# Odd layer of a hybrid trunk: the recurrences of two heads run together, 8 chunks per product stage

## The chip, the cores and the metric

The kernel runs on one core of a Trainium2 chip. The core's engines work from instruction queues of their own, each in its own order: TensorE (PE; its weight loads are shown as PEld), VectorE (DVE), ScalarE (ACT), GpSimd (POOL) and SyncE (SP), which here issues the DMA transfers. Engines wait for one another through semaphores. The metric is the device time of one launch in microseconds, lower is better.

## The reference, cut to what matters

Two layers on 512 tokens of width 1024, batch 1. The even layer (a short convolution beside a gated DeltaNet) and what follows each layer (output projection, LayerNorm, a gated embedding) stay as they are. The odd layer is an HGRN2 recurrence with 16 heads of width 128:

```python
q_raw, f_raw, i_in, z = jnp.split(x @ w_in, 4, axis=-1)
f = lower_bound + (1.0 - lower_bound) * jax.nn.sigmoid(f_raw)
q = jax.nn.silu(q_raw)
k = 1.0 - f
# per head: S_t = diag(f_t) S_{t-1} + k_t v_t^T,  o_t = S_t^T q_t,  with v = i_in
o = hgrn2_recurrence(q, k, i_in, log f)
o = rms_norm(o, hgrn_norm_g) * jax.nn.silu(z)
return o.reshape(bsz, s, 2048) @ w_out
```

## The kernel before

Everything is held feature-major: features on the 128 partitions, the 512 tokens (`S`) on the free axis. A weight chunk of 128 x 1024 (512 KB) is loaded by SP, then split into a high part (`whi`, ScalarE, L96) and a low part (`wlo`, VectorE, L97); three buffers of each (`chunk`). A dense product runs in three passes, hi*hi, hi*lo, lo*hi (`mm3`, L104 to L106). `proj` makes one 128 x 512 output of 8 such triples.

**The odd layer** goes head by head (`odd_layer`). `hgrn_front` projects f (`pf`) and q (`pq`), for every second head the values of two heads (`pi`, two chunks, token-major, 256 columns per product), and the output gate z (`pz`). `hgrn_core` then makes the attention inside each chunk of 128 tokens (`C`; four chunks, `NCH`) by doubling blocks, and the recurrence over chunks. Its TensorE work per head:

- `products` (L736), called three times (once on `q`, for B = 2 and 8 on `X`): inside each block of 32 tokens, keys times 48 columns, 16 products of 128 rows on 32 columns, at four column tiles in turn. The results `pw` are picked into `AD` by VectorE (L740).
- `pl` (L798), B = 32 and 64: four products per left block of each pair of blocks, on 32 or 64 columns; for B = 32 there are two left blocks (columns 0 and 64), each followed by a copy into `AT` (L799). A product of plain float32 shows as two instructions in the trace.
- three transposes `pkt` (L806), then per chunk the outputs `o` (L813, L814) and the state's increment `dS` (L817), all 128 wide.
- `head_norm`: squares, a normalisation, four transposes `pot` (L540), the gate, and the split into `yh` and `yl`.

Between them VectorE multiplies Q and k by the decays of ever larger blocks (`merge`, `total`, L719).

**Order.** The core is a generator. `start` queues it, and each triple of dense products calls `pump`, which emits the next stage once the number of triples that the stage yielded (`HG`; `HN` for the normalisation) has gone by. `drain` emits all that is left up to a head. So recurrence stages of one head are emitted between the dense triples of the next head's front. The framework's planner then sets each engine's final order, by what it takes to be ready first among emitted work, so a stage can end up later than emitted. On the chip each engine runs its queue in that order.

Of the kernel before, what the change touches and what calls it, by code (L numbers as in the profile page):

```python
"""Two-layer hybrid trunk (gated short convolution || gated DeltaNet, then HGRN2) on one core.

Everything is kept feature-major ([feature on partitions, token on the free axis]).  The large
products run as three float32r passes over exact hi/lo splits of both operands.
"""
# [17 lines left out]
P = 128  # L23
D = 1024
KD = D // P          # 8 feature tiles of the residual stream
S = 512
C = 128              # recurrence chunk
NCH = S // C
H = 8                # DeltaNet heads
HH = 16              # HGRN heads  # L30
# [7 lines left out]
HG = 5, 5, 2, 3, 2  # L38
# [5 lines left out]
# columns of the packed small parameters  # L44
# [3 lines left out]
class K:  # L48
    def __init__(self, tc, ctx, a):
# [4 lines left out]
        # work emitted between the steps of the dense products: [steps to wait, pieces]  # L54
# [21 lines left out]
    def po(self, name="po"):  # L76
        return self.ps.tile([P, 512], F32, tag="po", name=name, bufs=1)

    def chunk(self, src):
        """One weight chunk [128, 8, 128]: load, then split it exactly into hi + lo."""  # L80
        ch = self.chunk_tiles()
        self.chunk_part(ch, src, slice(0, 1024))
        return ch[1:]
# [15 lines left out]
    def mm3(self, ps, terms, first=True, last=True):  # L99
        """ps = sum over terms of (wh + wl)^T (xh + xl), without the lo*lo product."""  # L100
# [13 lines left out]
    def pump(self, units=1):  # L114
        """Emit what is due of the waiting work behind `units` more steps of dense products."""
# [15 lines left out]
    def drain(self, h=99, lanes=3):  # L131
        """Emit the waiting work of the heads up to h."""
# [6 lines left out]
    def rsqrt(self, pool, v, shape, tag):  # L139
        """1/sqrt(v) for v > 0: exponent-halving seed and three Newton steps."""  # L140
# [15 lines left out]
    def constants(self):  # L156
# [18 lines left out]
        # sums from the middle of the chunk, and from its start: [j, (2, i)]  # L175
        self.UCT = cp.tile([P, 2, P], F32, name="UCT")
        UC, UT = self.UCT[:, 0], self.UCT[:, 1]
        # [j, i] = 1 where j <= i
        sel(UT, self.ones, [[1, P]], ALU.is_ge, 0.0, base=0, channel_multiplier=-1)
        # [j, i] = 1 where j > i  # L180
# [3 lines left out]
        # columns i >= 64: 1 where 64 <= j <= i  # L184
        sel(UC[:, h:], UT[:, h:], [[0, h]], ALU.is_ge, 0.0, base=-h, channel_multiplier=1)
        # columns i < 64: -1 where i < j <= 63
# [4 lines left out]
        # 16-blocks: BO[p, q] = 1 where p and q share a block, MM[p, m] = 1 where p is its block's m-th,  # L191
        # HM[p, h] = 1 where p is in the h-th half of its 32-block, I32[p, i] = 1 where p is its 32-block's i-th
# [14 lines left out]
        # masks inside 32-blocks, over (chunk, pair of half blocks, column of the half block)  # L207
        def mask(B, lo, n):
            """1 where 2B pair + lo <= row < 2B pair + lo + n"""
# [7 lines left out]
            m = cp.tile([P, 64], U8, name=f"m{B}_{lo}_{n}")  # L217
            nc.vector.tensor_copy(m.rearrange("p (c i) -> p c i", c=NCH), t2.unsqueeze(1).to_broadcast([P, NCH, 16]))
            return m

        # row in the left block of the pair; in the right one; in the second and the first half of the left one
# [6 lines left out]
        # halved convolution taps (the other half of silu's (tanh + 1) / 2)  # L228
# [6 lines left out]
        # lower bound of the odd layer: softmax over depth, its cumulative sum less the first term  # L235
# [17 lines left out]
    def load_x(self, srcs):  # L253
        """x and the first weight chunks, in the order of use."""
# [460 lines left out]
    def hgrn_core(self, hp, h, f, k, q, vt, zg):  # L715
# [8 lines left out]
        def half4(t, B, side):  # L724
            return t.rearrange("p (k n s b) -> p k n s b", k=16, s=2, b=B)[:, :, :, side, :]
# [331 lines left out]
```

## Time and profile before

| | |
|---|---|
| runs | 1255.92, 1256.76, 1257.79 us; median 1256.76 us |
| span of the profiled execution | 1253.2 us (first to last instruction) |
| around the span, against the median | 3.6 us |
| odd layer's projections | 629.2 to 1087.7 us of the span |
| TensorE, VectorE, ScalarE busy | 99%, 67%, 46% of the span |

The profile is of one execution. The time of a run holds the span and what lies before its first and behind its last instruction; the profiled execution's own time is not given apart from its span, so the median of the runs stands for it. Matmuls are pipelined and their recorded lengths overlap, so TensorE's use is read from the starts of its instructions rather than from their lengths.

### The profile page before, as it was taken

Reading aid. Unit: us, or ns where it says so; the run is one execution under the profiler, and the core shown is the slowest. Engines: PE = TensorE matmul, PEld = TensorE weight load, DVE = VectorE, ACT = ScalarE, POOL = GpSimd, SP = SyncE. Lnnn points to the kernel's source line nnn. Section 1 sums busy time; section 2 is a strip of 40 time slices with the busy share of each in tenths; the row PEclk is TensorE's granted clock in tenths of the full one; section 3 lists DMA queues with packets and bytes.
Section 4 is the critical chain, followed back from the end, with each engine's and each line's share of the span. In section 5 each row is a group of like instructions: output and inputs, shape, how many; then the busy total and the mean of one; then the engine's idle time right before and its main releaser. Section 6 shows DMA issues by size and latency. Waiting matters only on the chain.

```text
span 1253.2 us, 24159 instructions
## 1 busy us (share of the span) xinstructions
PE 1236.9 (99%) x9590; PEld 1037.3 (83%) x9590; DVE 841.0 (67%) x2195; ACT 577.1 (46%) x1412; POOL 46.0 (4%) x76
## 2 busy tenths in 40 slices
PE   7999999999999999999999999999999999999998
PEld 6677877878787788898997878788887878779998
DVE  7778867676878754468646575757666665754784
ACT  4555545454555432237434454544444444532471
POOL 3000000000000000210000000000000000002100
PEclk9999999999999999999999999999999999999999
DMA  6322222221222222443432222122212122224422
GB/s 207 103 68 85 84 86 85 75 95 68 90 90 75 68 80 106 143 161 101 152 116 70 85 69 71 66 85 69 73 64 85 57 95 70 68 94 154 140 99 87
DMA packets 37313, 117.10 MB, mean 93 GB/s; under 512 B 4144, under 2 KB 8016, under 8 KB 37200
## 3 DMA queue, kind: packets, MB, share of 16 engines
q1 hardware_dynamic: 37200, 115.56, 27.0%
q8 instruction: 75, 1.23, 0.4%
q14 instruction: 38, 0.31, 0.1%
HBM read 111.32 MB, written 4.23 MB: 92 GB/s over the span
## 4 chain that ended last, share of the span: by engine, by line
PE 86%; DVE 7%; ACT 4%; DMA 1%; issue 1%; POOL 0%; SPq 0%; DVEq 0%; ACTq 0%; POOLq 0%
PE pz L104 5%; PE pz L105 5%; PE pz L106 5%; PE pout L104 4%; PE pout L106 4%; PE pout L105 4%; PE pi L104 3%; PE pq L104 3%; PE pf L104 3%; PE pi L105 3%; PE pqkv L105 2%; PE pi L106 2%; PE pqkv L106 2%; PE pqkv L104 2%; PE pf L105 2%; PE pq L105 2%
## 5 line engine op out<-in xcount | busy, mean ns | idle before, releaser
L97 DVE TENSOR_TENSOR wlo<-wraw,whi 128x1024 fp32r<-128x1024 f32 (+1 forms) x196 | 237.8, 1214 | 151.7 <-ACT whi L96 150.7
L96 ACT CAST whi<-wraw 128x1024 fp32r<-128x1024 f32 (+1 forms) x196 | 200.8, 1024 | 218.9 <-PE pout L105 77.6
L104 PE MATMUL pout<-yh,whi 128*128 128x256 f32 (+1 forms) x384 | 124.1, 323 | 0.0
L106 PE MATMUL pout<-yh,wlo 128*128 128x256 f32 (+1 forms) x384 | 123.4, 322 | 0.0
L105 PE MATMUL pout<-yl,whi 128*128 128x256 f32 (+1 forms) x384 | 123.0, 321 | 0.0
L104 PE MATMUL pz<-xh,whi 128*128 128x512 f32 x256 | 107.3, 419 | 0.2 <-DVE scr L401 0.2
L105 PE MATMUL pz<-xl,whi 128*128 128x512 f32 x256 | 102.2, 399 | 0.0
L106 PE MATMUL pz<-xh,wlo 128*128 128x512 f32 x256 | 101.0, 394 | 0.0
L104 PE MATMUL pqkv<-xh,whi 128*128 128x512 f32 x192 | 79.1, 412 | 4.8 <-ACT xh L152 4.8
L106 PE MATMUL pqkv<-xh,wlo 128*128 128x512 f32 x192 | 77.2, 402 | 2.0 <-DVE wlo L97 2.0
L105 PE MATMUL pqkv<-xl,whi 128*128 128x512 f32 x192 | 78.0, 406 | 0.0
L106 PEld LDWEIGHTS pout<-yh,wlo 128*128 128x128 f32 x384 | 72.5, 189 | 5.6
L104 PEld LDWEIGHTS pout<-yh,whi 128*128 128x128 f32 x384 | 72.3, 188 | 5.6 <-ACT yh L152 0.3
L105 PEld LDWEIGHTS pout<-yl,whi 128*128 128x128 f32 x384 | 72.2, 188 | 5.6 <-DVE yl L153 0.2
L104 PE MATMUL pi<-whi,xh 128*128 128x256 f32 x256 | 75.1, 293 | 0.0
L105 PE MATMUL pi<-wlo,xh 128*128 128x256 f32 x256 | 73.1, 285 | 0.0
L106 PE MATMUL pi<-whi,xl 128*128 128x256 f32 x256 | 72.3, 283 | 0.0
L105 PE MATMUL pgate<-x1l,whi 128*128 128x256 f32 x256 | 71.9, 283 | 0.4 <-DVE x1l L153 0.4
L104 PE MATMUL pgate<-x1h,whi 128*128 128x256 f32 x256 | 71.4, 283 | 0.6 <-ACT x1h L152 0.6
L106 PE MATMUL pgate<-x1h,wlo 128*128 128x256 f32 x256 | 71.5, 281 | 0.0
L719 DVE TENSOR_TENSOR Q<-Q,T 128x256 f32<-128x256 f32 x96 | 40.5, 422 | 33.2 <-PE pl L798 31.8
L106 PEld LDWEIGHTS pz<-xh,wlo 128*128 128x128 f32 x256 | 48.1, 188 | 10.0
(316 smaller groups left out, 2994.1 us busy)
## 6 DMA issues: line engine op xcount, KB each, us to landing
wraw<-in_we SPq DMA_DIRECT2D x62, 512.0 KB, 3.5
wraw<-in_wo SPq DMA_DIRECT2D x48, 512.0 KB, 3.5
wraw<-in_woe SPq DMA_DIRECT2D x21, 512.0 KB, 3.5
wraw<-in_woo SPq DMA_DIRECT2D x21, 512.0 KB, 3.5
wraw<-in_wg SPq DMA_DIRECT2D x16, 512.0 KB, 3.5
wraw<-in_wi SPq DMA_DIRECT2D x16, 512.0 KB, 3.5
gb<-drows SPq DMA_DIRECT2D x8, 512.0 KB, 3.9
xraw<-in_xT SPq DMA_DIRECT2D x8, 256.0 KB, 4.4
```

Source lines behind the costliest of these rows:

```text
L96: nc.scalar.copy(hi, raw)
L97: nc.vector.tensor_tensor(lo, raw, hi.bitcast(F32), op=SUB)
L104: nc.tensor.matmul(ps, wh, xh, start=first and i == 0, stop=False)
L105: nc.tensor.matmul(ps, wh, xl, start=False, stop=False)
L106: nc.tensor.matmul(ps, wl, xh, start=False, stop=last and i == n - 1)
L719: mul = lambda o, x, y: nc.vector.tensor_tensor(o, x, y, op=MUL)
```

## The change

Two heads are one unit (`g`). `hgrn_front` projects f of both heads and then q of both. Their common core is started, and `hgrn_values` projects the pair's values and both output gates behind it, so the core's stages are emitted between these products and those of the next pair's front. Every tile of the core holds both heads side by side: `G` = 8 chunks instead of 4, and operations of VectorE and ScalarE are twice as wide. `products` makes 32 products in one go, into a PSUM tile of its own (`pw`). For `pl`, all products of a stage are issued ahead of the copies, with the chunk as the outer and the left block as the inner loop. `X` has no tile of its own: the later columns are written into `q`. `k` is made at the core's start. `f`, `q`, `k`, `vt`, `zg`, `AD` and `AT` have one buffer where there were two (of half the size), and `o` two PSUM buffers for one. `HG` changes, and values call `pump` at each triple. `pair_norm` normalises both heads. The masks are made twice as wide, and the even layer reads their first half. Comments are taken out all over the file.

```diff
-HG = 5, 5, 2, 3, 2
+HG = 5, 8, 6, 4, 3
...
+        self.npo = 1
...
     def po(self, name="po"):
-        return self.ps.tile([P, 512], F32, tag="po", name=name, bufs=1)
+        return self.ps.tile([P, 512], F32, tag="po", name=name, bufs=self.npo)
+    def pw(self, name="pw"):
+        return self.ps.tile([P, 512], F32, tag="pw", name=name, bufs=1)
...
-            m = cp.tile([P, 64], U8, name=f"m{B}_{lo}_{n}")
-            nc.vector.tensor_copy(m.rearrange("p (c i) -> p c i", c=NCH), t2.unsqueeze(1).to_broadcast([P, NCH, 16]))
+            m = cp.tile([P, 2 * NCH * 16], U8, name=f"m{B}_{lo}_{n}")
+            nc.vector.tensor_copy(m.rearrange("p (c i) -> p c i", c=2 * NCH),
+                                  t2.unsqueeze(1).to_broadcast([P, 2 * NCH, 16]))
...
-    def hgrn_front(self, hp, h):
+    def hgrn_front(self, hp, g):
         nc, wo = self.nc, self.a["wo"]
...
+        f = hp.tile([P, 2 * S], F32, tag="f", name="f", bufs=1)
+        q = None
+        for j in range(2):
+            h = 2 * g + j
+            ps = self.acc("pf")
+            self.proj(wo[h], ps)
+            fj = f[:, j * S:(j + 1) * S]
+            nc.scalar.activation(fj, ps, AF.Tanh, scale=0.5)
+            nc.vector.tensor_scalar(fj, fj, self.fa[:, h:h + 1], self.fb[:, h:h + 1], op0=MUL, op1=ADD)
         v16 = lambda t: t.rearrange("p (n i) -> p n i", n=16)
...
+        for j in range(2):
+            h = 2 * g + j
+            ps = self.acc("pq")
+            self.proj(wo[HH + h], ps)
+            th = self.scr(hp)
+            nc.scalar.activation(th, ps, AF.Tanh, scale=0.5)
+            if q is None:
+                q = hp.tile([P, 32, 48], F32, tag="q", name="q", bufs=1)
+            nc.vector.scalar_tensor_tensor(q[:, 16 * j:16 * j + 16, :32], v16(th), 1.0, v16(ps), op0=ADD, op1=MUL)
+        return f, q
+    def hgrn_values(self, hp, g):
+        nc, wo = self.nc, self.a["wo"]
+        vt = hp.tile([P, NCH, 2 * C], F32, tag="vt", name="vt", bufs=1)
+        ws = [self.chunk(self.a["wi"][2 * g + i]) for i in range(2)]
+        ws = [(w[0].rearrange("p a b -> p (a b)").rearrange("p (k n) -> p k n", k=4),
+               w[1].rearrange("p a b -> p (a b)").rearrange("p (k n) -> p k n", k=4)) for w in ws]
+        for c2 in range(NCH // 2):
+            ps = self.acc("pi")
+            for j in range(2):
+                c = 2 * c2 + j
+                cs = slice(c * C, (c + 1) * C)
+                for k_ in range(KD):
                     self.mm3(ps[:, j * 2 * C:(j + 1) * 2 * C],
+                             [(self.xh[k_][:, cs], self.xl[k_][:, cs], ws[k_ // 4][0][:, k_ % 4], ws[k_ // 4][1][:, k_ % 4])],
+                             k_ == 0, k_ == KD - 1)
+                    self.pump(0.5)
+            nc.scalar.copy(vt[:, 2 * c2:2 * c2 + 2].rearrange("p c i -> p (c i)"), ps)
+        zg = hp.tile([P, 2 * S], F32, tag="zg", name="zg", bufs=1)
+        for j in range(2):
+            ps = self.acc("pz")
+            self.proj(wo[2 * HH + 2 * g + j], ps)
+            th = self.scr(hp)
+            nc.scalar.activation(th, ps, AF.Tanh, scale=0.5)
+            nc.vector.scalar_tensor_tensor(zg[:, j * S:(j + 1) * S], th, 1.0, ps, op0=ADD, op1=MUL)
+        return vt, zg
-    def hgrn_core(self, hp, h, f, k, q, vt, zg):
+    def hgrn_core(self, hp, g, f, q, late):
         nc = self.nc
+        G = 2 * NCH
         ck = lambda c: slice(c * C, (c + 1) * C)
-        v4 = lambda t: t.rearrange("p (c i) -> p c i", c=NCH)
+        v8 = lambda t: t.rearrange("p (c i) -> p c i", c=G)
         mul = lambda o, x, y: nc.vector.tensor_tensor(o, x, y, op=MUL)
...
         def half4(t, B, side):
-            return t.rearrange("p (k n s b) -> p k n s b", k=16, s=2, b=B)[:, :, :, side, :]
+            return t.rearrange("p (k n s b) -> p k n s b", k=32, s=2, b=B)[:, :, :, side, :]
...
         def products(X):
-            pa = self.pg("pw")[:, :NCH * 48].rearrange("p (c i) -> p c i", c=NCH)
-            for c in range(NCH):
+            pa = self.pw("pw")[:, :G * 48].rearrange("p (c i) -> p c i", c=G)
+            for c in range(G):
                 for b in range(4):
                     t0 = c * C + 32 * b
                     nc.tensor.matmul(pa[blk(b), c, :], k[:, t0:t0 + 32], X[:, 4 * c + b, :], start=True, stop=True)
...
         def pick(B, m, src):
             nc.vector.copy_predicated(AD.rearrange("p c (n s b) -> p c n s b", s=2, b=B)[:, :, :, 1, :],
-                                      m.rearrange("p (c n b) -> p c n b", c=NCH, b=B), src)
+                                      m.rearrange("p (c n b) -> p c n b", c=G, b=B), src)
         def merge(B, T, qs=True):
-            n = 256 // B
+            n = 512 // B
...
         def total(B, T):
             T2 = T.rearrange("p (n s) -> p n s", s=2)
-            Tn = hp.tile([P, 256 // B], F32, tag=f"T{B}", name=f"T{B}", bufs=1)
+            Tn = hp.tile([P, 512 // B], F32, tag=f"T{B}", name=f"T{B}", bufs=1)
             mul(Tn, T2[:, :, 0], T2[:, :, 1])
             return Tn
-        AD = hp.tile([P, NCH, 32], F32, tag="AD", name="AD", bufs=2)
-        Q = hp.tile([P, S], F32, tag="Q", name="Q", bufs=1)
-        v16 = lambda t: t.rearrange("p (n i) -> p n i", n=16)
-        mul(v16(Q), q[:, :, :32], v16(f))
+        AD = hp.tile([P, G, 32], F32, tag="AD", name="AD", bufs=1)
+        Q = hp.tile([P, 2 * S], F32, tag="Q", name="Q", bufs=1)
+        k = hp.tile([P, 2 * S], F32, tag="k", name="k", bufs=1)
+        v32 = lambda t: t.rearrange("p (n i) -> p n i", n=32)
+        nc.vector.tensor_scalar(k, f, -1.0, 1.0, op0=MUL, op1=ADD)
+        mul(v32(Q), q[:, :, :32], v32(f))
         nc.scalar.copy(q[:, :, 32:].unsqueeze(3), half4(Q, 1, 1))
         yield HG[0]
         pa = products(q)
-        mul(AD, pa[:, :, :32], self.I32.unsqueeze(1).to_broadcast([P, NCH, 32]))
+        mul(AD, pa[:, :, :32], self.I32.unsqueeze(1).to_broadcast([P, G, 32]))
         pick(1, self.mL[1], cols(pa, 2, 1))
         merge(1, f)
         T = total(1, f)
+        X = q
         for B in (2, 8):
-            X = hp.tile([P, 16, 48], F32, tag="X", name="X", bufs=1)
             nc.scalar.copy(cols(X, 0, B), half4(Q, B, 1))
             T2 = T.rearrange("p (n s) -> p n s", s=2)
-            mul(half(Q, B, 1), half(Q, B, 1), T2[:, :, 0:1].to_broadcast([P, 256 // B, B]))
+            mul(half(Q, B, 1), half(Q, B, 1), T2[:, :, 0:1].to_broadcast([P, 512 // B, B]))
             nc.scalar.copy(cols(X, 1, 2 * B), half4(Q, 2 * B, 1))
-            far = T.rearrange("p (k n s) -> p k n s", k=16, s=4)[:, :, :, 1:2]
-            mul(cols(X, 2, 2 * B), half4(Q, 2 * B, 1), far.to_broadcast([P, 16, 8 // B, 2 * B]))
+            far = T.rearrange("p (k n s) -> p k n s", k=32, s=4)[:, :, :, 1:2]
+            mul(cols(X, 2, 2 * B), half4(Q, 2 * B, 1), far.to_broadcast([P, 32, 8 // B, 2 * B]))
             yield HG[1]
...
+        self.freed = g
+        A4 = self.AT
         for b in range(4):
             nc.scalar.copy(A4[blk(b), :, blk(b)], AD[blk(b)])
         AT = A4.rearrange("p c i -> p (c i)")
         for B in (32, 64):
             yield HG[2]
-            k4, Q4 = v4(k), v4(Q)
-            p4 = v4(self.sm("pl"))
-            for l in range(0, C, 2 * B):
+            k8, Q8 = v8(k), v8(Q)
+            p8 = self.sm("pl")[:, :G * B].rearrange("p (c i) -> p c i", c=G)
+            left = range(0, C, 2 * B)
+            for c in range(G):
+                for l in left:
+                    ls, rs = slice(l, l + B), slice(l + B, l + 2 * B)
+                    nc.tensor.matmul(p8[ls, c, :], k8[:, c, ls], Q8[:, c, rs], start=True, stop=True)
+            for l in left:
                 ls, rs = slice(l, l + B), slice(l + B, l + 2 * B)
-                for c in range(NCH):
-                    nc.tensor.matmul(p4[ls, c, :B], k4[:, c, ls], Q4[:, c, rs], start=True, stop=True)
-                nc.scalar.copy(A4[ls, :, rs], p4[ls, :, :B])
+                nc.scalar.copy(A4[ls, :, rs], p8[ls, :, :])
             merge(B, T)
             T = total(B, T)
         yield HG[3]
-        kt = hp.tile([P, S], F32, tag="kt", name="kt", bufs=1)
-        pt = self.sm("pkt")
-        for c in range(NCH - 1):
-            nc.tensor.transpose(pt[:, ck(c)], k[:, ck(c)], self.ident)
-        nc.scalar.copy(kt[:, :3 * C], pt[:, :3 * C])
-        po = self.po("o")
+        kt = hp.tile([P, 2, 3 * C], F32, tag="kt", name="kt", bufs=1)
+        for j in range(2):
+            pt = self.sm("pkt")
+            for c in range(NCH - 1):
+                nc.tensor.transpose(pt[:, ck(c)], k[:, ck(NCH * j + c)], self.ident)
+            nc.scalar.copy(kt[:, j], pt[:, :3 * C])
+        po = [self.po("o") for _ in range(2)]
+        vt, zg = late
         St = None
         for c in range(NCH):
             yield HG[4]
-            if c > 0:
-                nc.tensor.matmul(po[:, ck(c)], Q[:, ck(c)], St, start=True, stop=False)
-            nc.tensor.matmul(po[:, ck(c)], AT[:, ck(c)], vt[:, c, :], start=c == 0, stop=True)
             if c < NCH - 1:
-                pd = self.sm("dS")
-                nc.tensor.matmul(pd[:, :C], kt[:, ck(c)], vt[:, c, :], start=True, stop=True)
-                Sn = hp.tile([P, C], F32, tag="S", name="S", bufs=2)
+                pd = self.sm("dS")[:, :2 * C].rearrange("p (j i) -> p j i", j=2)
+                Sn = hp.tile([P, 2, C], F32, tag="S", name="S", bufs=2)
+                for j in range(2):
+                    nc.tensor.matmul(pd[:, j], kt[:, j, ck(c)], vt[:, c, ck(j)], start=True, stop=True)
+            for j in range(2):
+                if c > 0:
+                    nc.tensor.matmul(po[j][:, ck(c)], Q[:, ck(NCH * j + c)], St[:, j], start=True, stop=False)
+                nc.tensor.matmul(po[j][:, ck(c)], AT[:, ck(NCH * j + c)], vt[:, c, ck(j)], start=c == 0, stop=True)
+            if c < NCH - 1:
                 if c == 0:
-                    nc.vector.tensor_copy(Sn, pd[:, :C])
+                    nc.vector.tensor_copy(Sn, pd)
                 else:
-                    nc.vector.scalar_tensor_tensor(Sn, St, T[:, c:c + 1], pd[:, :C], op0=MUL, op1=ADD)
+                    for j in range(2):
+                        nc.vector.scalar_tensor_tensor(Sn[:, j], St[:, j], T[:, NCH * j + c:NCH * j + c + 1], pd[:, j],
+                                                       op0=MUL, op1=ADD)
                 St = Sn
-        self.start(h, self.head_norm(hp, po, zg, h, 1, 0.25 / 128.0), 2)
+        self.start(g, self.pair_norm(hp, po, zg, g), 2)
+    def pair_norm(self, hp, po, zg, g):
+        nc, sp = self.nc, self.small
+        ck = lambda c: slice(c * C, (c + 1) * C)
+        v = sp.tile([P, 2 * NCH], F32, tag="pv", name="pv")
+        for j in range(2):
+            for c in range(NCH):
+                junk = hp.tile([P, C], F32, tag="junk", name="junk", bufs=2)
+                nc.scalar.activation(junk, po[j][:, ck(c)], AF.Square, accum_out=v[:, NCH * j + c:NCH * j + c + 1])
+        nc.vector.tensor_scalar(v, v, 0.25 / 128.0, NORM_EPS, op0=MUL, op1=ADD)
+        s = self.rsqrt(sp, v, [P, 2 * NCH], "pn")
+        os_ = [self.cs(hp) for _ in range(2)]
+        for j in range(2):
+            for c in range(NCH):
+                nc.scalar.mul(os_[j][:, ck(c)], po[j][:, ck(c)], s[:, NCH * j + c:NCH * j + c + 1])
+        yield HN
+        for j in range(2):
+            pt = self.sm("pot")
+            for c in range(NCH):
+                nc.tensor.transpose(pt[:, ck(c)], os_[j][:, ck(c)], self.ident)
+            y = os_[j]
+            nc.vector.scalar_tensor_tensor(y, pt, self.gn[:, 1:2], zg[:, j * S:(j + 1) * S], op0=MUL, op1=MUL)
+            self.split_to(self.yh[2 * g + j], self.yl[2 * g + j], y)
     def odd_layer(self):
         self.open_y(1)
+        self.npo = 2
         with self.tc.tile_pool(name="odd", bufs=1, reuse_waits="tile") as hp, self.psum("po") as self.ps:
-            self.AT = [hp.tile([P, NCH, C], F32, name=f"AT{i}") for i in range(2)]
-            for t in self.AT:
-                self.nc.gpsimd.memset(t, 0.0)
-            for h in range(HH):
-                fr = self.hgrn_front(hp, h)
-                self.drain(h - 1, 1)
-                self.start(h, self.hgrn_core(hp, h, *fr))
+            self.AT = hp.tile([P, 2 * NCH, C], F32, name="AT")
+            self.nc.gpsimd.memset(self.AT, 0.0)
+            for g in range(HH // 2):
+                f, q = self.hgrn_front(hp, g)
+                self.drain(g - 1)
+                late = []
+                self.start(g, self.hgrn_core(hp, g, f, q, late))
+                late.extend(self.hgrn_values(hp, g))
             self.drain()
```

## Rows read from the trace of the kernel before

**Rows 1.** Page, part 1: busy time, share of the span, instructions.

```profile
PE 1236.9 (99%) x9590; PEld 1037.3 (83%) x9590; DVE 841.0 (67%) x2195; ACT 577.1 (46%) x1412; POOL 46.0 (4%) x76
```

**Rows 2.** Waits of PE, 629 to 1124 us: total us, times, longest.

```profile
PE pot L540 <- ACT cs L535: 0.2, 1, 0.2
```

**Rows 3.** Windows: stretch, length, busy us of each engine, clock, DMA share, GB/s.

```profile
629.20:1087.70 458.50, 458.50 (x4108) 382.18 (x4108) 295.95 (x840) 206.20 (x507) 0.00 (x0) 1.00 0.23 75
```

**Rows 4.** Groups by form, PE: count, busy us, mean ns of one, idle before.

```profile
L736 PE MATMUL pw<-X,k 128*32 128x48 f32 x1024 | 17.5, 209 | 0.0
...
L798 PE MATMUL pl<-Q,k 128*32 128x32 f32 x256 | 14.0, 199 | 0.0
L798 PE MATMUL pl<-Q,k 128*64 128x64 f32 x128 | 10.9, 228 | 0.0
...
L736 PE MATMUL pw<-q,k 128*32 128x48 f32 x512 | 8.8, 209 | 0.0
```

**Rows 5.** Timeline of PE around a `pw` burst: start us, length us, instruction.

```profile
773.55 0.39 PE L104 MATMUL pf<-xh,whi 128*128 128x512 f32 x1
...
777.40 0.39 PE L106 MATMUL pf<-xh,wlo 128*128 128x512 f32 x1
777.72 0.55 PE L736 MATMUL pw<-q,k 128*32 128x48 f32 x32
778.20 0.50 PE L104 MATMUL pf<-xh,whi 128*128 128x512 f32 x1
778.53 0.40 PE L105 MATMUL pf<-xl,whi 128*128 128x512 f32 x1
```

**Rows 6.** Timeline of PE around two `pl` bursts of one head.

```profile
788.15 0.40 PE L106 MATMUL pz<-xh,wlo 128*128 128x512 f32 x1
788.48 0.44 PE L798 MATMUL pl<-Q,k 128*32 128x32 f32 x8
788.85 0.50 PE L104 MATMUL pz<-xh,whi 128*128 128x512 f32 x1
789.18 0.40 PE L105 MATMUL pz<-xl,whi 128*128 128x512 f32 x1
...
791.61 0.40 PE L104 MATMUL pz<-xh,whi 128*128 128x512 f32 x1
791.94 0.68 PE L798 MATMUL pl<-Q,k 128*64 128x64 f32 x8
792.54 0.50 PE L105 MATMUL pz<-xl,whi 128*128 128x512 f32 x1
792.88 0.40 PE L106 MATMUL pz<-xh,wlo 128*128 128x512 f32 x1
```

**Rows 7.** Timeline of PE around four 128-wide transposes.

```profile
783.79 0.60 PE L540 MATMUL pot<-ident,cs 128*128 128x128 f32 x4
...
784.46 0.40 PE L105 MATMUL pq<-xl,whi 128*128 128x512 f32 x1
```

**Rows 8.** Timeline of PE, even layer: 16 instructions, and a burst of 64.

```profile
80.31 0.44 PE L622 MATMUL T<-N,GA 32*32 32x32 f32 x16
...
219.32 0.25 PE L606 MATMUL DD<-T,W 32*32 32x16 f32 x8
...
219.59 0.23 PE L606 MATMUL DD<-T,W 32*32 32x16 f32 x7
...
219.82 0.23 PE L609 MATMUL DD<-W,T 32*32 32x16 f32 x6
```

**Rows 9.** Groups by form, DVE: count, busy us, mean ns of one, idle before.

```profile
L719 DVE TENSOR_TENSOR Q<-Q,T 128x256 f32<-128x256 f32 x96 | 40.5, 422 | 33.2 <-PE pl L798 31.8 <-ACT X L772 0.5 <-DVE hnt L147 0.4
...
L719 DVE TENSOR_TENSOR Q<-q,f 128x512 f32<-128x512 f32 x16 | 11.1, 692 | 11.4 <-PE o L813 11.3
```

**Rows 10.** Waits of all engines, longest in total first.

```profile
DVE Q L719 <- PE pl L798: 31.8, 31, 2.3
...
ACT X L772 <- PE pw L736: 12.0, 15, 1.3
```

More of the change, by code (lines that the diff above doesn't have):

```diff
@@ L553, in inverse @@
         blk = lambda q: slice(32 * q, 32 * q + 32)
-        v16 = lambda m: m.rearrange("p (c i) -> p c i", c=NCH)
+        v16 = lambda m: m[:, :NCH * 16].rearrange("p (c i) -> p c i", c=NCH)
         g32 = hp.tile([P, NCH, 32], F32, tag="g32", name="g32", bufs=1)
@@ L673, in even_layer @@
             self.drain()
-    def hgrn_front(self, hp, h):
+    def hgrn_front(self, hp, g):
         nc, wo = self.nc, self.a["wo"]
-        ps = self.acc("pf")
-        self.proj(wo[h], ps)
-        f = hp.tile([P, S], F32, tag="f", name="f", bufs=2)
-        nc.scalar.activation(f, ps, AF.Tanh, scale=0.5)
-        nc.vector.tensor_scalar(f, f, self.fa[:, h:h + 1], self.fb[:, h:h + 1], op0=MUL, op1=ADD)
-        k = hp.tile([P, S], F32, tag="k", name="k", bufs=2)
-        nc.vector.tensor_scalar(k, f, -1.0, 1.0, op0=MUL, op1=ADD)
-        ps = self.acc("pq")
-        self.proj(wo[HH + h], ps)
-        th = self.scr(hp)
-        nc.scalar.activation(th, ps, AF.Tanh, scale=0.5)
-        q = hp.tile([P, 16, 48], F32, tag="q", name="q", bufs=2)
-        v16 = lambda t: t.rearrange("p (n i) -> p n i", n=16)
-        nc.vector.scalar_tensor_tensor(q[:, :, :32], v16(th), 1.0, v16(ps), op0=ADD, op1=MUL)
-        if h % 2 == 0:
-            self.vt = hp.tile([P, NCH, 2 * C], F32, tag="vt", name="vt", bufs=2)
-            ws = [self.chunk(self.a["wi"][h + i]) for i in range(2)]
-            ws = [(w[0].rearrange("p a b -> p (a b)").rearrange("p (k n) -> p k n", k=4),
-                   w[1].rearrange("p a b -> p (a b)").rearrange("p (k n) -> p k n", k=4)) for w in ws]
-            for c2 in range(NCH // 2):
-                ps = self.acc("pi")
-                for j in range(2):
-                    c = 2 * c2 + j
-                    cs = slice(c * C, (c + 1) * C)
-                    self.mm3(ps[:, j * 2 * C:(j + 1) * 2 * C],
-                             [(self.xh[k_][:, cs], self.xl[k_][:, cs], ws[k_ // 4][0][:, k_ % 4], ws[k_ // 4][1][:, k_ % 4])
-                              for k_ in range(KD)])
-                    self.pump(4)
-                nc.scalar.copy(self.vt[:, 2 * c2:2 * c2 + 2].rearrange("p c i -> p (c i)"), ps)
-        vt = self.vt[:, :, (h % 2) * C:(h % 2 + 1) * C]
-        ps = self.acc("pz")
-        self.proj(wo[2 * HH + h], ps)
-        self.drain(h - 2)
-        return f, k, q, vt, self.silu2(hp, ps, "zg")
@@ L786, in hgrn_core @@
             T = total(2 * B, T)
-        A4 = self.AT[h % 2]
+        self.freed = g
+        A4 = self.AT
         for b in range(4):
```

## Prediction

> **What bounds the kernel now.** I read the page's busy times first: TensorE is busy for 99% of the span, VectorE for 67% [rows 1]. A busy TensorE need not be one at its peak, so the next question is whether it waits. The waits of PE in the odd layer name one, 0.2 us [rows 2]. The windows view of the stretch in which the layer's projections run (629.2 to 1087.7 us) says the same: busy 458.50 of 458.50 us at a granted clock of 1.00, which is the 2.4 GHz level, with a DMA share of 0.23 [rows 3]. So the layer lasts as long as TensorE's own instruction stream, and a change is worth what it takes out of that stream or what waits it puts in.
>
> The stream has two kinds of work: dense products of 512 or 256 columns, and the recurrence's small products set between them. The groups by form give the second kind's counts [rows 4]: 1024 + 512 instructions of `pw`, in bursts of 32 (16 products, each issued as two instructions), so 48 bursts, three per head; 256 of `pl` on 32 columns and 128 on 64, in bursts of 8, so 32 and 16 bursts. The busy times in these rows don't say what a burst costs, for neighbours overlap in them. For that I read starts in the timeline.
>
> Undisturbed dense products start 0.2265 us apart: 17 steps from 773.55 to 777.40 [rows 5]. Around a `pw` burst, the second dense product behind it (778.53) starts 1.13 us after the last one ahead of it (777.40). Two steps would be 0.453, so the burst costs 0.677 us. Its 32 starts are spread over 0.55 − 0.209 (the mean of one, [rows 4]) = 0.341 us, 11 ns apart, 0.352 us for 32. The remaining 0.325 us is a price of going in and out: the dense product behind is 0.33 us from its successor, and there is a gap ahead of the burst [rows 5].
>
> The same for `pl` [rows 6]. On 32 columns: 789.18 − 788.15 = 1.03, less 0.453, is 0.577 us; starts (0.44 − 0.199)/7 = 34 ns apart, so 0.275 for eight, and 0.302 for in and out. On 64 columns: 792.88 − 791.61 − 0.453 = 0.817; starts (0.68 − 0.228)/7 = 65 ns apart, 0.517 for eight, and 0.300 for in and out.
>
> Bursts over the whole array don't pay it: the four transposes `pot` put off the next dense pair by 784.46 − 783.79 − 0.2265 = 0.44 us, 0.11 each [rows 7]. So I count `pw` and `pl` bursts alone.
>
> **The change, part by part.** *Products, 8 chunks at a time.* Per pair of heads, before: six bursts of 32. After: three of 64. The instructions stay; three times 0.325 us goes: 0.98 us per pair, for eight pairs 7.8 us.
>
> *`pl` on 32 columns.* Before: four bursts of 8 per pair, 4 × 0.577 = 2.31 us; the two halves of a head stand apart because a copy by ScalarE is emitted between them. After: all 32 instructions come ahead of the copies, in one burst, and the loop alternates between column tiles 0 and 64. No row of before shows these products alternating. Lower bound of the step between starts: 11 ns, that of `pw` with its four column tiles [rows 5]. Upper bound: the present 34 ns [rows 6]. I take the even layer's `T` products, 16 instructions of the same 32 × 32 size alternating between two tiles: (0.44 − 0.199)/15 = 16 ns, with the mean of one `pl` for its last [rows 4, 8]; it is nearest in size and in number of tiles. So 32 × 0.016 + 0.302 = 0.81 us, and 1.49 us per pair goes, 11.9 us in all. The bounds give 0.65 and 1.39 us, 13.2 and 7.4 us in all.
>
> *`pl` on 64 columns.* One column tile either way, so only one of two in-and-out prices goes: 0.30 us per pair, 2.4 us.
>
> *The 128-wide bursts* (`o`, `dS`, `pkt`, `pot`) keep their instructions, 0.11 us each [rows 7]; joined in pairs they save nothing I can price, at most some hundredths of a us a burst.
>
> *VectorE and ScalarE.* Operations double in size and halve in number. A product of 256 columns takes 422 ns, one of 512 692 ns [rows 9], under twice, so VectorE's load falls. That is worth nothing while the dense products cover it; if they didn't, it would be a small gain too.
>
> *Moved projections and loads.* The order of weight chunks on SP's queue becomes f f q q i i z z instead of f q i i z f q z: the same eight loads per pair through the same three buffers, at a DMA share of 0.23 [rows 3]. Splits of chunks wait for buffers that TensorE frees, as they do now, and TensorE never waits for them in this layer [rows 2]. Zero.
>
> *Single buffers.* I count in steps of three dense products, 0.68 us. The pair's core starts at 0; its stages come at 5, 13, 21, 27, 33, 37, 40, 43, 46 and 49; values and gates end at 32, the next pair's f at 48, its q at 64. `f` is last read at 5 and next written at 40; `q` at 21 and 56; `k` at 37 and 64; `Q`, `vt` and `AT` at 49 and past 64; `zg` at 64 and past 80. No reuse falls due before its last reader. Zero. At the layer's end there is more cover than now, since the last core starts before the values and not behind the gate.
>
> *Columns written over q.* `X` has no tile any more; ScalarE's copies and one product write the next columns into `q`, so they must wait for the `pw` burst that reads it, now for each of the two later product stages, today only for the last (12.0 us in 15 waits of ScalarE, [rows 10]). Between a burst and the next, 8 steps or 5.4 us apart, VectorE has five 512-wide products (3.5 us at 0.69, [rows 9]) and some picks and short products, about 1 us, and ScalarE a last copy, some 0.7: 5.2 us, an estimate. Behind the waiting copy on ScalarE's queue stand splits of weight chunks, which are a chunk or two ahead of TensorE. Zero, with little to spare; the stall that it could become is among the rivals.
>
> *Masks* double in width: small copies at the start, off the path.
>
> Sum: 7.8 + 11.9 + 2.4 = 22.1 us. The profiled execution has a span of 1253.2 us and its runs a median of 1256.76, so 3.6 us lie around the span and stay. 1256.8 − 22.1 = 1234.7; I say 1235.
>
> **The rivals.** *No concurrency between two column tiles.* `pl` stays at 34 ns, the gain is 7.8 + 7.4 + 2.4 = 17.6 us, the time 1239. For it: all 128 rows are used in every tile. Against it: so they are in `pw`, whose four column tiles start 11 ns apart where one tile alone needs 34 [rows 5, 6]. 12%. The Trainium skill (TensorE: Matmul & The Clock Gate, "The mechanism") has weight loads overlap matmuls in flight only where the row group differs, which would make this rival the result. The trace's `pw` rows speak against that rule.
>
> *Long bursts outrun the queue.* If the second half of a 64-burst fell from 11 to 34 ns, it would cost 32 × 0.023 × 24 = 17.7 us and leave 4.4: 1252. For it: in the even layer's burst of 64, loads run less far ahead in the second half. Against it: starts there are 0.27/32 = 8.4 ns apart in the first half and (219.82 − 219.59)/26 = 8.8 ns in the second [rows 8], still under the 11 that `pw` needs. 4%. The Trainium skill (same page, "Architectural detail: the array is 16× 32×32, not 1× 128×128") gives TensorE a reorder window of 64, which such a burst would leave; the even layer's rows show how little that costs.
>
> *Slower: the first stage of each pair comes too late.* Today a head's q is done well before its core starts; after the change the core starts right behind the second q. Behind its last product lie, in a chain: tanh, q, k and Q over 1024 columns, and a copy. At 0.69 us per 512 columns [rows 9] that is 0.69 × (1 + 1 + 2 + 2 + 1) = 4.8 us, an upper estimate, and the previous pair's two gated outputs can lie in between. The first products are due after 5 steps, 3.4 us. If TensorE stood for the rest, 1.4 us per pair, that would cost 11 us, and with 2.9 us of outputs in between (four operations of some 0.7 us) 34 us: 1269. It decides from 22.1/8 = 2.8 us per pair on. Against it: the order of instructions isn't the emission order but is planned by readiness (a `pl` burst stands inside a triple of dense products, between L104 and L105, [rows 6]), dense products of values and gates are always there to fill, and today VectorE waits 31.8 us for `pl` on TensorE [rows 10] while TensorE waits 0.2 [rows 2]. 6%.
>
> *A smaller stall*, there or at the columns written over `q`, of up to 1 us per pair costs up to 8 us: up to 1243. 12%.
>
> **How the numbers follow.** Forecast 1235 us: 66%, own range 1230 to 1239 (lower end: 11 ns for `pl` and a us or two of joined 128-wide bursts; upper end: 34 ns). Then 12, 4, 6 and 12% in the order of the rivals. A change of 0.2% (2.5 us) is about what a measurement of this kernel can tell from none. The range 1229 to 1247 leaves out the long-burst case, most of the slow one, and part of the small stalls. Faster: all but the slow case and part of the long-burst case, 92%; same 3%; slower 5%.
>
> **What would show it.** Right: `pw` in bursts of 64 that cost about 1.03 us, `pl` on 32 columns in bursts of 32 at some 16 ns, bursts of 16 on 64 columns at about 1.33 us, the window of the layer's projections some 20 us shorter, and PE waits near zero. Wrong: a wait of PE for `q`, `X` or `cs` in every pair, bursts cut in two by dense products, a step that grows inside a burst, or `pl` at 34 ns.

## The result, and the profile after

The kernel after takes 1228.26 us (median of four runs, 1227.49 to 1230.07). The kernel before, with a fourth run of 1254.28 us beside the three known ones, has a median of 1256.34 us. The ratio is 0.978, with a 95% interval of 0.9766 to 0.9794: 28 us faster. The forecast of 1235 us had the direction and the mechanism; the time fell 0.7 us under the low end of its range, 1229.

The profiled run of after took 1228.52 us, of which 1226.8 are its span. Part 1 of its page, which answers to [rows 1]:

```profile
PE 1210.2 (99%) x9590; PEld 1029.8 (84%) x9590; DVE 805.0 (66%) x1835; ACT 560.4 (46%) x1316; POOL 45.9 (4%) x75
```

TensorE has the same 9590 instructions. VectorE and ScalarE have 360 and 96 fewer, those of the core twice as wide. The waits of PE from 620 us to the end, which answer to [rows 2]:

```profile
PE ppl L110 <- DVE wlo L101: 0.8, 1, 0.8
PE pgate L109 <- DVE x1l L157: 0.2, 1, 0.2
```

Both lie in the tail behind the odd layer. In the layer itself TensorE waits for nothing, although VectorE and ScalarE wait for it, as they did in [rows 10]. Waits of all engines, 640 to 1070 us:

```profile
ACT q L794 <- PE pw L756: 28.0, 9, 3.4
...
DVE AD L760 <- PE pw L756: 27.1, 16, 2.5
```

These cost nothing, since TensorE has dense products to issue. To compare the layers I take a stretch with the same work in both kernels: from the first product of `pf` to the 200th of `pout`. In the windows view of before it is

```profile
629.15:1143.30 514.15, 513.95 (x4474) 425.59 (x4473) 324.54 (x911) 225.34 (x555) 4.90 (x4) 1.00 0.23 78
```

and of after

```profile
628.22:1118.77 490.55, 490.42 (x4475) 422.49 (x4473) 288.82 (x552) 208.34 (x459) 4.83 (x4) 1.00 0.26 82
```

The columns are length, busy time and count of PE, PEld, DVE, ACT and POOL, granted clock, DMA share, GB/s. The same work of TensorE (4471 starts in both; the windows also count what reaches in from outside), at the same clock, takes 23.6 us less. The span is 26.4 us shorter, so 2.8 lie elsewhere.

The bursts show where the 23.6 us come from. Timeline of PE in after, around a `pw` burst and the two `pl` bursts of one pair (start, length, instruction; against [rows 5, 6]):

```profile
723.02 0.39 PE L110 MATMUL pz<-xh,wlo 128*128 128x512 f32 x1
723.34 0.89 PE L756 MATMUL pw<-q,k 128*32 128x48 f32 x64
724.16 0.50 PE L108 MATMUL pz<-xh,whi 128*128 128x512 f32 x1
724.50 0.40 PE L109 MATMUL pz<-xl,whi 128*128 128x512 f32 x1
...
728.14 0.39 PE L110 MATMUL pz<-xh,wlo 128*128 128x512 f32 x1
728.46 0.70 PE L822 MATMUL pl<-Q,k 128*32 128x32 f32 x32
729.09 0.50 PE L108 MATMUL pz<-xh,whi 128*128 128x512 f32 x1
729.43 0.39 PE L109 MATMUL pz<-xl,whi 128*128 128x512 f32 x1
...
733.08 0.39 PE L110 MATMUL pf<-xh,wlo 128*128 128x512 f32 x1
733.40 1.15 PE L822 MATMUL pl<-Q,k 128*64 128x64 f32 x16
734.47 0.50 PE L108 MATMUL pf<-xh,whi 128*128 128x512 f32 x1
734.81 0.39 PE L109 MATMUL pf<-xl,whi 128*128 128x512 f32 x1
```

Read as in the prediction, the second dense start behind a burst less the last one ahead of it, less two steps of 0.2265: `pw` 724.50 − 723.02 − 0.453 = 1.027 us, `pl` on 32 columns 729.43 − 728.14 − 0.453 = 0.837, on 64 columns 734.81 − 733.08 − 0.453 = 1.277. Summed over the whole stretch, as the excess over dense steps of 226.7 ns (512 columns) and 120.0 ns (256 columns), where each burst also takes what the dense products behind it lose up to the next burst:

| | before | after | difference | forecast |
|---|---|---|---|---|
| `pw` | 48 bursts, 32.8 us | 24, 24.6 us | −8.2 | −7.8 |
| `pl`, both widths | 48 bursts, 31.6 us | 8 + 8, 17.2 us | −14.4 | −14.3 |
| `o`, `dS`, `pkt`, `pot` | 51.9 us | 50.9 us | −1.0 | about 0 |

The rows add up to the 23.6 us. The last row is less plain than it seems. With only the next two dense products counted, as the prediction reads a burst, its bursts cost 49.2 us before and 49.4 after, so joining them gave nothing by that reading. All bursts together fell by 22.4 us in it; the other 1.2 us lie in dense products further behind. Behind a `pw` burst of before, the second to fifth step between dense products took 235, 229, 233 and 230 ns on the mean, and only then 227. Such visits to the small products number 181 before and 92 after.

Outside the odd layer's stretch the code is the same, but for the masks' first half, and yet the tail behind the even layer, from its 193rd `pout` product to the first `pf`, takes 104.5 us for 107.3, and the rest behind the odd layer's 200th `pout` 1.8 us less; the start-up, to the 65th dense product, takes 1.8 us more, but 0.2 more in another profile of the same kernel (a_last, below). Together with the 23.6 us these make up the 26.4. The dense products on 256 columns have become faster. Windows of PE over 207 products of `pout` in a row, before:

```profile
1142.46:1167.18 24.72, 24.72 (x207) 1.00 0.48 171
```

and after:

```profile
1117.94:1141.98 24.04, 24.04 (x207) 1.00 0.58 176
```

Over 206 steps that is 120.0 ns a step before and 116.7 after, at a granted clock of 1.00 in both. Shapes, order and loops of these products are untouched.

### The profile page after: what moved, and what is told of

The parts are those of the page before. It is cut to its first block, busy times and chain, and to the rows that moved or that the text cites. A ratio compares the mean times of both kernels' runs of the same rounds, so it can differ in the third digit from the quotient of the medians.

```text
span 1226.8 us, 23658 instructions
## 1 busy us (share of the span) xinstructions
PE 1210.2 (99%) x9590; PEld 1029.8 (84%) x9590; DVE 805.0 (66%) x1835; ACT 560.4 (46%) x1316; POOL 45.9 (4%) x75
## 4 chain that ended last, share of the span: by engine, by line
PE 88%; DVE 6%; ACT 3%; issue 1%; DMA 1%; SPq 0%; POOL 0%; POOLq 0%; DVEq 0%; ACTq 0%
PE pz L108 5%; PE pz L109 5%; PE pz L110 5%; PE pout L110 4%; PE pout L108 4%; PE pout L109 4%; PE pqkv L109 3%; PE pqkv L110 3%; PE pqkv L108 3%; PE pi L109 3%; PE pi L108 3%; PE pi L110 2%; PE pf L108 2%; PE pf L110 2%; PE pf L109 2%; PE pq L110 2%
## 5 line engine op out<-in xcount | busy, mean ns | idle before, releaser
L108 PE MATMUL pz<-xh,whi 128*128 128x512 f32 x256 | 103.8, 405 | 0.0
L108 PEld LDWEIGHTS pz<-xh,whi 128*128 128x128 f32 x256 | 48.1, 188 | 9.3
```

What stands on the lines that cost most here:

```text
L108: nc.tensor.matmul(ps, wh, xh, start=first and i == 0, stop=False)
```

## The experiments

Three questions: are the 22 us made by what the prediction says; what makes the rest; is there a stall? Every kernel was timed against the kernel before on its own chip (medians 1255.38, 1254.67 and 1255.6 us in three groups).

**A full-array instruction inside each `pw` burst (a_cut).** To after, one transpose of the identity into unused columns of `pw`, between the two halves:

```diff
+            pt = self.pw("pw")
+            pa = pt[:, :G * 48].rearrange("p (c i) -> p c i", c=G)
             for c in range(G):
+                if c == NCH:
+                    nc.tensor.transpose(pt[:, G * 48:], self.ident, self.ident)
```

> The changed kernel with one 128-wide transpose of the identity (into columns of the same PSUM tile that nothing reads) between the two halves of each of the 24 bursts of pw. Theory 1 (each entry into and exit from products on part of the array costs 0.325 us, however long the burst): 24 x (0.325 + 0.11) = 10.4 us more than the changed kernel, and a burst with its cut costs 1.03 + 0.435 = 1.46 us. Rival (the price belongs to the dense neighbours of a burst, not to the switch): only the transposes, 24 x 0.11 = 2.6 us more.

Measured: 1237.99 us (1237.31 to 1239.73), ratio to before 0.9862 [0.9847, 0.9877]. Timeline of its PE at one burst:

```profile
725.18 0.39 PE L110 MATMUL pz<-xh,wlo 128*128 128x512 f32 x1
725.50 0.55 PE L759 MATMUL pw<-q,k 128*32 128x48 f32 x32
725.98 0.33 PE L756 MATMUL pw<-ident 128*128 128x128 f32 x1
726.23 0.55 PE L759 MATMUL pw<-q,k 128*32 128x48 f32 x32
726.71 0.50 PE L108 MATMUL pz<-xh,whi 128*128 128x512 f32 x1
727.05 0.40 PE L109 MATMUL pz<-xl,whi 128*128 128x512 f32 x1
```

The burst costs 1.432 us on the mean of 24, for 1.027: 0.405 us for one cut, 9.7 us in all, where the transpose itself is worth 0.11 [rows 7]. The time is 9.0 us above that of after in the same group (a_again, below). So a visit from the whole array to column tiles and back has a price of its own, some 0.3 us, and joining bursts takes it out. The weight loads of after show where it arises:

```profile
722.80 0.19 PEld L110 LDWEIGHTS pz<-xh,wlo 128*128 128x128 f32 x1
723.34 0.75 PEld L756 LDWEIGHTS pw<-q,k 128*32 128x32 f32 x64 [0.35 <-issue]
724.16 0.19 PEld L108 LDWEIGHTS pz<-xh,whi 128*128 128x128 f32 x1
```

The load of the last dense product starts 0.22 us ahead of its product (722.80 for 723.02 above); that of the first `pw` product, and that of the first dense one behind the burst, start no earlier than the products themselves (723.34 and 724.16). Ahead of a burst of 128-wide products the load keeps its lead, 0.23 us on the median. The Trainium skill (TensorEngine Tiling (Array Packing), "Key Properties") says that changing the tiling mode drains TensorE; this trace agrees, with loads that lose their lead at both changes, and puts about 0.3 us beside it.

**The order of `pl`, in both kernels (a_pl_lc, b_pl).** After with the loops exchanged (one column tile at a time, still one burst), and before with only the new order of `pl`:

```diff
 # a_pl_lc
-            for c in range(G):
-                for l in left:
+            for l in left:
+                for c in range(G):
 # b_pl
-            for l in range(0, C, 2 * B):
-                ls, rs = slice(l, l + B), slice(l + B, l + 2 * B)
-                for c in range(NCH):
+            left = range(0, C, 2 * B)
+            for c in range(NCH):
+                for l in left:
+                    ls, rs = slice(l, l + B), slice(l + B, l + 2 * B)
                     nc.tensor.matmul(p4[ls, c, :B], k4[:, c, ls], Q4[:, c, rs], start=True, stop=True)
+            for l in left:
+                ls, rs = slice(l, l + B), slice(l + B, l + 2 * B)
                 nc.scalar.copy(A4[ls, :, rs], p4[ls, :, :B])
```

> The changed kernel with the two loops around pl exchanged: still one burst of 32 instructions on 32 columns, but first all chunks on column tile 0, then all on column tile 64, so that column tiles no longer alternate. Theory 1 (two column tiles run side by side only where they alternate): starts 32 to 34 ns apart instead of 16, 8 x 32 x 0.017 = 4.4 us more than the changed kernel. Rival (one burst is all that matters): the same time as the changed kernel within 1 us.

> The kernel before, head by head, with only the order of pl changed as the change has it: all products of a stage ahead of the copies, chunk outside, left block inside. Per head two bursts of 8 on 32 columns become one of 16 that alternates between two column tiles. Theory 1 (0.302 us in and out, 16 ns a step): 2 x 0.577 - (0.302 + 16 x 0.016) = 0.596 us a head, 9.5 us in all, about 1246 us. Rival (no two column tiles side by side): 0.31 us a head, 4.9 us, about 1250.5 us.

Measured: a_pl_lc 1232.09 us (1230.79 to 1234.05), 0.9815 [0.9801, 0.9828]; b_pl 1245.94 us (1245.22 to 1246.3), 0.9931 [0.9917, 0.9944]. Timeline of a_pl_lc:

```profile
727.90 0.39 PE L110 MATMUL pz<-xh,wlo 128*128 128x512 f32 x1
728.22 1.10 PE L822 MATMUL pl<-Q,k 128*32 128x32 f32 x32
729.25 0.50 PE L108 MATMUL pz<-xh,whi 128*128 128x512 f32 x1
729.58 0.39 PE L109 MATMUL pz<-xl,whi 128*128 128x512 f32 x1
```

The 32 starts spread over (1.10 − 0.2)/31 = 29 ns each, for (0.70 − 0.2)/31 = 16 in after; the burst costs 0.40 us more on the mean, 3.2 us over eight, less than the 4.4 that was expected from a step of 32 to 34 ns. Same instructions, same burst, other order: the step falls to 16 ns only where the column tiles alternate. In b_pl the first half of the idea stands alone:

```profile
728.55 0.40 PE L106 MATMUL pz<-xh,wlo 128*128 128x512 f32 x1
728.88 0.45 PE L799 MATMUL pl<-Q,k 128*32 128x32 f32 x16
729.25 0.50 PE L104 MATMUL pz<-xh,whi 128*128 128x512 f32 x1
729.59 0.40 PE L105 MATMUL pz<-xl,whi 128*128 128x512 f32 x1
```

Sixteen instructions cost 0.587 us here, what eight cost in [rows 6] (0.577). Its odd-layer stretch is 9.2 us shorter than that of before, its time 8.7. So nearly a third of the whole gain needs neither pairs of heads nor wider tiles.

**The masks alone, and room alone (b_masks, b_pad64).** Among the constants, which are set ahead of the even layer, the change makes only the masks larger: 64 bytes more per partition for each of nine. b_masks makes them so in the kernel before and reads their first half; b_pad64 leaves the masks and sets 64 unused bytes aside behind the constants:

```diff
 # b_masks
-            m = cp.tile([P, 64], U8, name=f"m{B}_{lo}_{n}")
+            m = cp.tile([P, 2 * NCH * 16], U8, name=f"m{B}_{lo}_{n}")
 # b_pad64
+        nc.gpsimd.memset(cp.tile([P, 64], U8, name="room"), 0)
```

> The kernel before with only the masks made twice as wide, as the change makes them; every tile that is allocated behind them (weight chunks, activations) then lies 576 bytes further on, while the tiles at the other end of the memory stay. Theory A (place): the 256-column products of pout and pgate step at 116 to 117 ns instead of 119 to 120 because of where the operands lie; over their 1536 instructions that is 4 to 5 us, so about 1251 to 1252 us where before has 1256. Theory B (a matter of the run or the chip, not of the kernel): the step stays at 119 to 120 ns and the time within 1 us of before.

> The kernel before with nothing but 64 bytes per partition set aside behind the constants, so that weight chunks and activations lie 64 bytes further on against the y tiles and the second half's x1 tiles at the other end of the memory. Theory A (place; distances matter modulo 128 bytes, and the masks' 576 bytes are 64 over a multiple of that): the same steps as with the wide masks, 117 ns for the 256-column pout and for the second half of pgate, some 2.7 us less than before. Rival (the masks themselves, or another modulus): 120 ns and the time of before.

Measured: b_masks 1252.64 us (1251.11 to 1253.87), 0.9978 [0.9969, 0.9987]; b_pad64 1251.9 us (1251.13 to 1254.47), 0.9984 [0.9975, 0.9992]. The same window of PE in b_pad64 (b_masks has the same 24.04):

```profile
1140.46:1164.50 24.04, 24.04 (x207) 1.00 0.52 176
```

Unused room does what the masks do, so it is the place of the tiles behind them: 116.7 ns a step for 120.0, and 2.7 or 2.8 us of the time against the median of before in the same group. By the ratios that is 2.8 us (1.6 to 3.9) for b_masks and 2.0 (1.0 to 3.1) for b_pad64. The two tails are 3.1 us shorter in the traces of both, and the odd layer's stretch differs from that of before by under 0.2. Of the 4 to 5 us expected, the rest is not there, for the `pgate` products of the tails came down only from 119.5 to 117.8 ns a step in their long run of 310; in after they take 116.0.

**More room in after (a_pad64, a_pad96).** The same line in after, with 64 and with 96 bytes, tests whether the distance between operands sets the step.

> The changed kernel with 64 bytes per partition set aside behind the constants; distances to the other end of the memory are again those of the kernel before modulo 128 bytes. Theory A: the 256-column pout back at 120 ns (768 x 3.3 ns) and the second half of pgate back at 119.5 (384 x 2.3 ns), some 3.4 us more than the changed kernel, about 1232 us. Rival (another modulus, or chance): as the changed kernel, 1229 us.

> The changed kernel with 96 bytes per partition set aside behind the constants; the distance between weight chunk and y, and between weight chunk and the second half's x1, is then 64 over a multiple of 128 bytes, as the distance to the first half's x1 is in the changed kernel, whose products step at 113.5 ns. Theory A: 113.5 ns for these too, 1152 x 3.5 ns = 4 us less than the changed kernel, about 1225 us. Rival: no gain, 1229 us or more.

Measured: a_pad64 1229.53 us (1227.68 to 1231.08), 0.98 [0.9787, 0.9813]; a_pad96 1228.49 us (1226.95 to 1229.97), 0.9792 [0.9779, 0.9805]. The step of a_pad64 in this window is 118.4 ns, neither the 120.0 of before that the rule of distances forecast nor the 116.7 of after, so that rule fell. That of a_pad96 is 113.4:

```profile
1118.14:1141.50 23.36, 23.36 (x207) 1.00 0.53 178
```

Of the 4 us expected nothing came. The `pgate` products kept their 116 ns, and the step of 113.4 ns, worth 1.3 us over the 384 `pout` products of this tail, went for the most part into waits, of which this tail has 1.1 us more than in after. The largest new one stands behind the last product of the window:

```profile
1141.50 0.28 PE L110 MATMUL pout<-yh,wlo 128*128 128x256 f32 x1
1142.36 0.70 PE L955 MATMUL mu<-racc,onesD 128*128 128x256 f32 x2 [0.58 <-POOL racc L934]
```

TensorE, some 0.7 us ahead, waits 0.58 us for GpSimd's sums, for which it doesn't wait in after. In the tail the next engine stands right behind.

**Earlier due stages, and a tile for X (a_hg, a_x, a_last).** After with the later product stages due after 5 triples, not 8; after with X as a tile of its own; after itself.

```diff
 # a_hg
-HG = 5, 8, 6, 4, 3
+HG = 5, 5, 6, 6, 3
 # a_x
-        X = q
         for B in (2, 8):
+            X = hp.tile([P, 32, 48], F32, tag="X", name="X", bufs=1)
```

> The kernel after, with its second and third product stage due after 5 dense steps of 0.68 us instead of 8 (HG = 5, 5, 6, 6, 3). This tries the rival of a small stall at the columns written over `q`: between two bursts VectorE and ScalarE have some 5.2 us of work by my estimate, and 5 steps are 3.4 us. Theory 1 (the place at which a burst stands is planned by readiness, so a burst that is due too early is set later and dense triples fill in): the time of after, 1228 to 1230 us, PE without waits for q, and the distance between the bursts of a pair stays above 5 us. Theory 2 (the burst stands where it is due and TensorE stands for what is lacking): 5.2 - 3.4 = 1.8 us for two stages of eight pairs, 29 us, 1257 us, with a wait of PE for ACT or DVE on q in each pair; a third of it, 1238, if my 5.2 us is too high by 1.2.

> The kernel after, with a tile X of its own for the columns of the second and third product stage, as before, instead of writing them over `q`. Theory 1 (the copies that wait for the burst that reads `q` are covered by dense products): no change, 1228 to 1230 us, while the waits of ScalarE and VectorE for `pw` on TensorE shrink. Theory 2 (the waits that the sharing brings do cost): up to 1 us per pair less, 1221 us. A third way: the tile moves others in SBUF, and the step of 256-column products changes by some us in either direction; the odd layer's stretch tells it apart, for it has next to no such products beside the values.

> The kernel after, once more, as the reference beside the two runs of this call: 1228 to 1230 us.

Measured: a_hg 1228.91 us (1228.06 to 1229.7), a_x 1228.92 (1228.78 to 1230.03), a_last 1228.54 (1227.66 to 1230.49); ratios 0.9789 [0.9775, 0.9804], 0.9792 [0.9777, 0.9806] and 0.979 [0.9774, 0.9806]. No change in either. Timeline of PE in a_hg, the bursts of one pair:

```profile
710.74 0.89 PE L756 MATMUL pw<-q,k 128*32 128x48 f32 x64
...
715.35 0.89 PE L756 MATMUL pw<-q,k 128*32 128x48 f32 x64
...
720.79 0.89 PE L756 MATMUL pw<-q,k 128*32 128x48 f32 x64
```

They stand 4.61 and 5.44 us apart, for 5.93 and 6.92 in after, and PE's only wait of the layer is

```profile
PE pot L878 <- ACT cs L873: 0.2, 1, 0.2
```

So my 5.2 us for the chain between two bursts was too high, and the first theory's clause that the distance stays above 5 us missed: after has over a microsecond to spare there. In a_x the waits did not shrink either (ScalarE waits 27.2 us in 8 for `pw`, 28.0 in 9 in after): the wait for the third stage exists with a tile of its own too, and the second stage's copies come after the burst that reads `q` anyway.

After ran once more in the first group (a_again):

> The changed kernel once more, on the same chip as the runs beside it. Theory A (place): 256-column products of pout and pgate step at 116 to 117 ns again, 1228 us. Theory B (run or chip): the step can be 120 ns this time, and the time then some 5 us higher, 1233 us.

Measured: 1228.99 us (1228.78 to 1231.56), 0.9793 [0.978, 0.9807]. The same 207 `pout` products step at 116.7 ns again, not at 120; in a_last, the same kernel too, they take 117.8.

## Where the prediction was right, and where it failed

**Joined `pw` bursts: right.** 1.027 us a burst, for 1.03 in the prediction. a_cut shows the price by putting it back. The sum came to 8.2 us for 7.8.

**`pl`: right, in step and sum.** 16 ns and 0.85 us a burst on the mean, for 16 and 0.81. 14.4 us measured, 14.3 forecast. a_pl_lc and b_pl show that the order does it. The rival without concurrency between two tiles is out, and with it, for these products, the Trainium skill's rule that weight loads overlap only where the row group differs (TensorE: Matmul & The Clock Gate, "The mechanism"): all of these use all rows.

**Long bursts don't outrun the queue.** The starts of a `pw` burst of 64 are 11.0 ns apart in its first half and 10.2 in its second, on the mean of 24, so the rival by the window of 64 (the Trainium skill, same page, "Architectural detail: the array is 16× 32×32, not 1× 128×128") is out at this length.

**No stall.** Neither the first stage of a pair, nor the columns over `q`, nor single buffers cost anything: no PE wait in the layer, and a_hg and a_x leave the time where it was.

**What failed: "Masks double in width: small copies at the start, off the path".** This put the masks at nothing. The copies are off the path; the width is not. It moves what lies behind the masks in SBUF, and with it the step of the 256-column products of both tails. I costed instructions and not addresses. That is 2.7 us (b_masks), outside everything that the sum had, and alone more than the 0.7 us by which the range was missed. In after the two tails are 4.6 us shorter, not 3.1 as in b_masks. What makes the further 1.5 us was not tested. A candidate that the code shows is the pair's norm, which adds three tiles of 32 bytes, two buffers each, to a pool that is opened ahead of both layers.

**The second: "3.6 us lie around the span and stay".** The base mixed the span of one execution with the median of others. Every run whose own span is on record, of before and of after, has 1.7 us around it (1.66 to 1.80), so the profiled execution of before stands for a run of some 1254.9 us and not 1256.8: the base was 1.9 us too high. The medians of the later groups of before, 1254.7 to 1255.6, agree.

**The third: what a visit costs behind its second dense product.** The odd layer's stretch gave 23.6 us for 22.1. The bursts, read as the prediction reads them, gave 22.4; 1.2 us come from dense products further behind, as the section on the result shows. The prediction let a visit end at the second dense product. Its "at most some hundredths of a us a burst" for the 128-wide ones was in the text and in the range, and not in the sum.

**Taken together.** 1234.7 − 1.9 (base) − 1.5 (odd layer) − 4.6 (tails) + 1.8 (start-up) = 1228.5 us, and the profiled run of after took 1228.52. The mechanism of the 22 us was right. The range was missed by the base and by terms that stood at nothing: its own low end took 11 ns for `pl` and a us or two of joined 128-wide bursts, and neither that nor the 1229 had anything for work outside the layer or for the base. That the miss was as small as 0.7 us is in part luck, since the start-up took back 1.8 us for reasons not found.

**Open.** What in the placement sets the step of these products was not found: a rule by distance failed in a_pad64. What the change moves besides the masks was not taken alone. Why the start-up differs between profiles by up to 2 us, among those of the same kernel too, was not followed.

## What to carry to other kernels

Where TensorE is full and never waits, look for changes between column-tiled and full-array work among its instructions: each visit cost 0.3 us here, for bursts of 8 to 64 instructions, so make visits fewer and longer, and inside one alternate the column tiles (16 ns for 29 an instruction). Before pairing heads, try the order alone: b_pl got 8.7 us with six lines. And when a constant's size changes, read the step of dense products that the diff doesn't touch, for a few bytes can move it by 3%.

## What the runs showed of the hardware

The step of the same 256-column product, at a granted clock of 1.00, depended on the bytes added per partition ahead of its operands. It was 120.0 ns in before, 116.7 with 64 (b_pad64) or with the masks' 576 (b_masks, after), 118.4 with 64 more than after and 113.4 with 96 more. The place alone doesn't fix it: one group of `pgate` products behind the even layer ran at 113.5 ns a step in the profile of after and at 117.8 in that of a_again, the same kernel. In the odd layer the products of 512 columns kept their 226.7 ns, well behind a burst, in before and after. Those of `pz` in the even layer did not: 227.5 ns on the mean in before, 228.7 in after, and why was not followed.
